# Stick-breaking masks as one row of four bf16 products ahead of the logits, and the bias tables' one-hot products as one row of three

## The chip, the cores and the metric

The kernel runs on one core of a Trainium2 chip. A core has a matrix engine (TensorE; the profile calls its products PE and its weight loads PEld), a vector engine (DVE), a scalar engine (ACT), GpSimd (POOL) and SyncE (SP), which issues transfers; POOL issues transfers too. The metric is the device time of one execution in microseconds (us); smaller is better. Each time is given beside runs of the kernel before on the same chip.

## The reference, cut to what matters

The program is one layer of a hybrid decoder over 512 tokens of width 1024: an input projection, three causal attention branches, gates, an output projection, a LayerNorm, a squared-ReLU MLP and a second LayerNorm. Two pieces of it are touched.

The stick-breaking branch has 8 heads of 64 columns. With z the scaled logits of query t and key s:

```python
before = k_pos[None, :] < q_pos[:, None]
log_keep = jnp.where(before, jax.nn.log_sigmoid(-z), 0.0)
later = lax.cumsum(log_keep, axis=3, reverse=True) - log_keep
a = jnp.where(before, jnp.exp(jax.nn.log_sigmoid(z) + later), 0.0)
```

The other two branches add a relative bias: a table `rel_bias` (32 buckets, 16 heads) is looked up at the bucket of the distance between query and key.

## The kernel before, in words

All large products run in a three-product form: a float32 operand is split into a high part, rounded to the format fp32r that TensorE takes, and a low part (the rest); high·high, high·low and low·high are summed in a bank of PSUM. The weights stream in through a ring: a DMA on SP (L213) brings raw rows, ACT casts the high part (`wh`, L243), DVE subtracts for the low part (`wl`, L245), and the projection items (`t_item`, `mm3`, L87 to L89) consume them. Two PSUM banks (`mm_bank`) alternate between items; six banks (`at_bank`) serve attention.

The main loop (L1965) walks over the items. Before an item's products, and once more in the middle of them, `step()` (L1937) advances the attention heads, which are Python generators, and then the pending generators, among them `tables()`. This gives the order in which instructions are written down; a planner of the framework then orders each engine's queue and allots buffers out of free pools, by data dependences and this order. `issue_after` adds ordering by hand in a few places.

**A stick-breaking head** (`sb_head`, L1601) takes three banks and writes four blocks of keys into them: block 3 (256 columns) and block 2 (256) share a bank, block 1 (384) and block 0 (512) have one each. For each block, from the last to the first, it issues the logits as two fp32r products (`mm_pair`, L146 and L147) and then one bf16 product identity × mask (L1613 with 256 columns for block 3, L1616 with 128 columns for the others), which adds -1e30 above the diagonal. So bf16 and fp32r products alternate. After that ACT and DVE form the log terms of each bank (L1628 to L1654), triangle and all-ones products add the sums over later keys in place (L1661, L1665), ACT takes the exponential (L1671), and value products write a fresh bank (L1684, L1686), which L1692 and L1693 take out. Eight heads run between 20 us and 229 us.

**The bias tables** (`rel_vec`, L1480, driven by `tables`, L1519): `make_lam` (L1562, at item 10) writes the bias table split into three bf16 parts, plus a row of -1e30, as `rel` (97 rows x 16). `load_onehot` brings three one-hot matrices `oh` (97 x 512, bf16). Five products follow, one in each step: `rel` columns of one head group (97 x 4) by 512, 128, 384, 256 and 256 columns of `oh` (L1483), each into a bank of its own, each copied out by ACT (L1485, 4 rows) and sent to a DRAM strip `rv` by a POOL DMA (L1486). Then `shifted` (L1489) reads `rv` back as shifted tables (L1495), and `turned` (L1505) reverses them at item 22.

Of the kernel before, what the change touches and what calls it, by code (L numbers as in the profile page):

```python
# [12 lines left out]
BF16 = mybir.dt.bfloat16  # L13
# [3 lines left out]
S = 512  # L17
D = 1024
P = 128
# [36 lines left out]
def trunk(tc, a, out):  # L56
    nc = tc.nc
    es = ExitStack()
    with es:
# [10 lines left out]
        def nm(s):  # L70
            uid[0] += 1
            return f"{s}_{uid[0]}"

        def slot(name, dt=F32):
            return big.tile([P, 512], dt, name=nm(name), tag="s", bufs=NSLOT)
# [4 lines left out]
        def mm_bank():  # L80
            return psum.tile([P, 512], F32, name=nm("mm"), tag="mm", bufs=2)

        def at_bank():
            return psum.tile([P, 512], F32, name=nm("at"), tag="at", bufs=6)
# [58 lines left out]
        def mm_pair(ps, st, tw, side, cs, cm, start, stop):  # L143

            hi, lo = tw[side]
            nc.tensor.matmul(ps, st[side][:, cs], hi[:, cm], start=start, stop=False, skip_group_check=True)  # L146
            nc.tensor.matmul(ps, st[side][:, cs], lo[:, cm], start=False, stop=stop, skip_group_check=True)  # L147
# [137 lines left out]
        T = {}  # L285
# [1162 lines left out]
        identb = one.tile([P, P], BF16, name="identb")  # L1448
# [13 lines left out]
        mask_b = one.tile([P, 2, P], BF16, name="mask_b")  # L1462
# [13 lines left out]
        rel = one.tile([97, 16], BF16, name="rel")  # L1476
        nc.vector.memset(rel[96:97, :], NEG)
        rv = dram.tile([16, 640], F32, name="rv")

        def rel_vec(cols, segs):  # L1480
            for src, d0, n in segs:
                ps = at_bank()
                nc.tensor.matmul(ps[0:4, :n], rel[:, cols], src, start=True, stop=True)  # L1483
                sb = slot("rvs")[0:4, :]
                nc.scalar.copy(sb[:, :n], ps[0:4, :n])  # L1485
                nc.gpsimd.dma_start(rv[cols, d0:d0 + n], sb[:, :n])  # L1486
                yield

        def shifted(h0, n, m):  # L1489
            ts = []  # L1490
            per = 512 // m
            for i in range(0, n, per):
                t = slot("sh")
                s = rv[h0 + i:h0 + i + 1, 0:1]
                nc.gpsimd.dma_start(t.rearrange("p (h m) -> p h m", m=m),  # L1495
                                    bass.AP(tensor=s.tensor, offset=s.offset,
                                            ap=[[1, P], [640, per], [1, m]]))
                ts.append(t)
            return ts, m
# [10 lines left out]
        tab_da = tab_g0 = tab_g1 = tab_g2 = None  # L1510

        oh = []

        def load_onehot():
            oh.extend(slot("oh", BF16) for _ in range(3))
            for i in range(3):
                nc.gpsimd.dma_start(oh[i][:97, :], a["onehot"][:, 512 * i:512 * i + 512])

        def tables():  # L1519
            nonlocal tab_g0, tab_g1, tab_g2  # L1520
            yield from rel_vec(slice(0, 4), [(oh[0][:97, :], 0, 512), (oh[1][:97, 0:128], 512, 128)])
            yield from rel_vec(slice(4, 8), [(oh[1][:97, 128:512], 0, 384)])
            yield from rel_vec(slice(8, 12), [(oh[2][:97, 0:256], 0, 256)])
            yield from rel_vec(slice(12, 16), [(oh[2][:97, 256:512], 0, 256)])
            tab_g0 = shifted(4, 4, 256)
            tab_g1 = shifted(8, 4, 128)
            tab_g2 = shifted(12, 4, 128)
# [34 lines left out]
        def make_lam():  # L1562
            lamt, t, r = lams

            nc.vector.tensor_copy(rel[0:32, :], t)
            nc.vector.tensor_sub(t, t, rel[0:32, :])
            nc.vector.tensor_copy(rel[32:64, :], t)
            nc.vector.tensor_copy(r, rel[32:64, :])
            nc.vector.tensor_sub(t, t, r)
            nc.vector.tensor_copy(rel[64:96, :], t)  # L1570
            lp = one.tile([P, 2], F32, name="lp")
            for i in range(2):
                nc.vector.scalar_tensor_tensor(lamt[:, 2 * i, :], lamt[:, 2 * i, :], 1.0, lamt[:, 2 * i + 1, :],
                                               op0=OP.mult, op1=OP.mult, accum_out=lp[:, i:i + 1])
            nc.scalar.activation(lp, lp, AF.Exp)
            nc.vector.tensor_sub(lam, lp[:, 0:1], lp[:, 1:2])
            nc.vector.tensor_scalar(lam, lam, LAM_INIT, -1.0, op0=OP.add, op1=OP.mult)
            nc.vector.tensor_scalar(gcol, gcol, 1.0 - LAM_INIT, None, op0=OP.mult)
# [22 lines left out]
        def sb_head(hd):  # L1601
            pr, side = hd // 2, hd % 2
# [3 lines left out]
            blk = [(0, 0, 0, 512), (1, 1, 0, 384), (2, 2, 0, 256), (3, 2, 256, 256)]  # L1606
            bank = [at_bank() for _ in range(3)]
            for kb, bi, c0, n in reversed(blk):
                ps = bank[bi][:, c0:c0 + n]
                mm_pair(ps, T["sb_k", pr], T["sb_q", pr], side, slice(kb * P, kb * P + P), slice(S - n, S),  # L1610
                        kb != 2, False)
                if kb == 3:
                    nc.tensor.matmul(ps, identb, mask_b.rearrange("p a b -> p (a b)"), start=False, stop=False,  # L1613
                                     skip_group_check=True)
                else:
                    nc.tensor.matmul(ps[:, 0:P], identb, mask_b[:, 1, :], start=False, stop=False,  # L1616
                                     skip_group_check=True)
            w = [512, 384, 512]
            sph, spl, later = {}, {}, {}
            for bi in (2, 1, 0):  # L1620
                n = w[bi]
                ps = bank[bi][:, :n]
# [35 lines left out]
            for kb, bi, c0, n in reversed(blk):  # L1658
                ps = bank[bi][:, c0:c0 + n]
                for hl in (sph, spl):  # L1660
                    nc.tensor.matmul(ps, tri_r, hl[bi][:, c0:c0 + n], start=False, stop=False, skip_group_check=True)  # L1661
                if kb < 3:
                    n2, hl = later[kb]
                    for t in hl:
                        nc.tensor.matmul(bank[bi][:, c0 + n - n2:c0 + n], ones_r, t, start=False, stop=False,  # L1665
                                         skip_group_check=True)
                if kb == 3:
                    continue
                n = w[bi]
# [12 lines left out]
            for kb, bi, c0, n in blk:  # L1682
                v = V["sb_v", 0, kb][hd // 4][:, hd % 4]
                nc.tensor.matmul(po[:, S - n:S], v.rearrange("p two d -> p (two d)"), ah[bi][:, c0:c0 + n],  # L1684
                                 start=kb == 0, stop=False, skip_group_check=True)
                nc.tensor.matmul(po[A, S - n:S], v[:, 0, :], al[bi][:, c0:c0 + n], start=False, stop=kb == 3,  # L1686
                                 skip_group_check=True)
# [233 lines left out]
        for hd in range(8):  # L1921
            waiting.append((3, sb_head(hd), SB_PERIOD))
# [42 lines left out]
        for n, it in enumerate(items):  # L1965
# [31 lines left out]
            if n == 10:  # L1997
                with tc.issue_after(st["low"]):
                    make_lam()
            if n == 9:  # L2000
                load_onehot()
            if n == 13:
                pending.append(tables())
# [33 lines left out]
            ps = it["bank"]() if it["bank"] else mm_bank()  # L2037
# [115 lines left out]
```

## Time and profile before

| what | value |
|---|---|
| time, median of 3 runs | 1042.58 us (1042.33 to 1043.28) |
| the profiled execution's own time | 1043.19 us |
| its span | 1041.0 us |
| TensorE products | 5450, each with a weight load of its own |
| share of the span, PE / PEld / DVE / ACT / POOL | 99% / 85% / 76% / 57% / 17% |
| mean granted TensorE clock | 0.998 of full speed |
| moved by DMA | 249.21 MB, mean 239 GB/s |

The span is what the profiler recorded between the first and the last instruction; 2.2 us of the execution lie outside it. A product's recorded duration is modelled and overlaps with the next one's (0.39 us for 512 columns, while one starts every 0.23 us), so what a product costs is read from the distance between starts, not from its duration. In rows of the timeline the first number is the start and the second the duration, both in us; then come engine, line, operation, output <- inputs, the tile (contraction rows * output rows), and the moved operand with its type. A wait that ended at another instruction stands in brackets.

### The profile page before, as it was taken

What the parts mean: (1) busy time and instruction counts of PE and PEld (TensorE: products, weight loads), DVE (VectorE), ACT (ScalarE), POOL (GpSimd) and SP (SyncE); (2) the same over time, 40 slices, a digit from 0 to 9 for tenths busy, and PEclk for the clock granted to TensorE, in tenths of its full rate; (3) what the DMA queues carried; (4) which work ended last, traced back from release to release, by engine and by line L of the source; (5) the groups of instructions that cost most, each with busy time, mean ns of one, the idle gap of its engine ahead of it and who ended that gap; (6) DMA issues with size and microseconds to landing.
All of it is one profiled execution on the core that took longest, in us unless ns stands there. A gap on an engine that the chain in (4) does not pass through costs nothing.

```text
span 1041.0 us, 15056 instructions
## 1 busy us (share of the span) xinstructions
PE 1031.1 (99%) x5450; PEld 880.1 (85%) x5450; DVE 787.0 (76%) x1408; ACT 593.2 (57%) x1014; POOL 180.0 (17%) x271
## 2 busy tenths in 40 slices
PE   9999999999999999999999999999999999999997
PEld 6888788889888888888888888889999889889886
DVE  6888577769774667779788895798768877877966
ACT  7566445536344545676575743775666556555651
POOL 0003412031211232411011040111111111111001
PEclk9999999999999999999999999999999999999999
DMA  8449978495985999967889795479999999999612
GB/s 308 121 154 271 255 214 197 128 283 142 278 207 206 258 281 294 248 199 202 251 238 230 269 320 197 147 219 331 320 288 316 296 316 314 306 344 286 201 59 81
DMA packets 71323, 249.21 MB, mean 239 GB/s; under 512 B 8809, under 2 KB 9593, under 8 KB 71249
## 3 DMA queue, kind: packets, MB, share of 16 engines
q0 software_dynamic: 32464, 116.21, 44.7%
q1 hardware_dynamic: 38208, 131.13, 35.2%
q8 instruction: 43, 0.70, 0.3%
q10 hardware_dynamic: 576, 0.92, 0.2%
q14 instruction: 32, 0.25, 0.1%
HBM read 246.10 MB, written 98.59 MB: 331 GB/s over the span
## 4 chain that ended last, share of the span: by engine, by line
PE 94%; DVE 2%; ACT 2%; issue 1%; DMA 0%; POOL 0%; DVEq 0%; POOLq 0%
PE mm L87 10%; PE mm L88 10%; PE mm L89 10%; PE at L1261 4%; PE at L1262 4%; PE at L1263 4%; PE at L599 3%; PE at L601 3%; PE at L600 3%; PE mm L496 2%; PE mm L498 2%; PE mm L497 2%; PE at L89 1%; PE at L87 1%; PE at L88 1%; PE at L761 1%
## 5 line engine op out<-in xcount | busy, mean ns | idle before, releaser
L243 ACT CAST wh<-raw 128x1024 fp32r<-128x1024 f32 x257 | 268.7, 1049 | 241.1 <-PE mm L88 133.6
L245 DVE TENSOR_TENSOR wl<-raw,wh 128x1024 fp32r<-128x1024 f32 x257 | 312.5, 1222 | 112.2 <-ACT wh L243 110.9
L87 PE MATMUL mm<-xhT,wh 128*128 128x512 f32 x302 | 120.0, 397 | 0.0
L89 PE MATMUL mm<-xhT,wl 128*128 128x512 f32 x302 | 118.3, 392 | 0.0
L88 PE MATMUL mm<-xlT,wh 128*128 128x512 f32 x302 | 118.2, 391 | 0.0
L87 PE MATMUL mm<-x1hT,wh 128*128 128x256 f32 x256 | 73.8, 288 | 0.0
L1261 PE MATMUL at<-wh,hh 128*128 128x512 f32 x188 | 73.7, 392 | 0.0
L1262 PE MATMUL at<-wl,hh 128*128 128x512 f32 x188 | 73.7, 392 | 0.0
L1263 PE MATMUL at<-wh,hl 128*128 128x512 f32 x188 | 73.1, 389 | 0.0
L88 PE MATMUL mm<-x1lT,wh 128*128 128x256 f32 x256 | 72.2, 283 | 0.0
L89 PE MATMUL mm<-x1hT,wl 128*128 128x256 f32 x256 | 71.8, 283 | 0.0
L89 PEld LDWEIGHTS mm<-xhT,wl 128*128 128x128 f32 x302 | 56.8, 188 | 12.0
L87 PEld LDWEIGHTS mm<-xhT,wh 128*128 128x128 f32 x302 | 56.8, 188 | 11.3 <-issue 0.4
L88 PEld LDWEIGHTS mm<-xlT,wh 128*128 128x128 f32 x302 | 56.8, 188 | 10.5
L87 PEld LDWEIGHTS mm<-x1hT,wh 128*128 128x128 f32 x256 | 48.8, 190 | 4.8 <-ACT up L1195 2.9
L88 PEld LDWEIGHTS mm<-x1lT,wh 128*128 128x128 f32 x256 | 48.9, 191 | 1.5
L89 PEld LDWEIGHTS mm<-x1hT,wl 128*128 128x128 f32 x256 | 48.6, 191 | 0.0
L1095 POOL DMA_DIRECT2D usum<-in_wu_dram x32 | 28.5, 928 | 103.1 <-DVE wl L245 38.7
L1095 POOL DMA_DIRECT2D dsum<-in_wd_dram x28 | 25.5, 933 | 100.2 <-DVE wl L245 33.3
L1263 PEld LDWEIGHTS at<-wh,hl 128*128 128x128 f32 x188 | 35.3, 188 | 7.6
L1261 PEld LDWEIGHTS at<-wh,hh 128*128 128x128 f32 x188 | 35.5, 189 | 6.0
L1262 PEld LDWEIGHTS at<-wl,hh 128*128 128x128 f32 x188 | 35.5, 189 | 5.6
(601 smaller groups left out, 2686.4 us busy)
## 6 DMA issues: line engine op xcount, KB each, us to landing
usum<-in_wu_dram POOLq DMA_DIRECT2D x48, 512.0 KB, 9.2
dsum<-in_wd_dram POOLq DMA_DIRECT2D x42, 512.0 KB, 9.1
raw<-in_wt_dram SPq DMA_DIRECT2D x38, 512.0 KB, 5.7
raw<-usum SPq DMA_DIRECT2D x32, 512.0 KB, 7.8
raw<-dsum SPq DMA_DIRECT2D x28, 512.0 KB, 8.1
raw<-in_wd_dram SPq DMA_DIRECT2D x25, 512.0 KB, 6.5
raw<-in_wu_dram SPq DMA_DIRECT2D x24, 512.0 KB, 7.2
raw<-in_wv_dram SPq DMA_DIRECT2D x18, 512.0 KB, 5.5
```

The lines of the kernel that those rows point to most:

```text
L87: nc.tensor.matmul(ps, wh, xh, start=start, stop=False, skip_group_check=True)
L88: nc.tensor.matmul(ps, wh, xl, start=False, stop=False, skip_group_check=True)
L89: nc.tensor.matmul(ps, wl, xh, start=False, stop=stop, skip_group_check=True)
L243: i = nc.scalar.copy(h, raw)
L245: i = nc.vector.tensor_sub(lo, raw, h.bitcast(F32))
L599: nc.tensor.matmul(ps, h[:, q], c["h"][:, n], start=go, stop=False, skip_group_check=True)
L600: nc.tensor.matmul(ps, h[:, q], c["l"][:, n], start=False, stop=False, skip_group_check=True)
L601: nc.tensor.matmul(ps, lo[:, q], c["h"][:, n], start=False, stop=end, skip_group_check=True)
L1095: i = nc.gpsimd.dma_start(o, i, accum_op=OP.add, max_dma_last_dim=4096)
L1261: nc.tensor.matmul(ps, h[:, q], c["h"][:, s], start=go, stop=False, skip_group_check=True)
L1262: nc.tensor.matmul(ps, h[:, q], c["l"][:, s], start=False, stop=False, skip_group_check=True)
L1263: nc.tensor.matmul(ps, lo[:, q], c["h"][:, s], start=False, stop=end, skip_group_check=True)
```

## The change

In `sb_head` the four mask products are issued first, in a row, into the still empty banks (the first one of each bank now clears it), and the eight logit products follow and add to them. The products and their shapes are the same.

The five one-hot products become three in a row into one bank. Their stationary operand is a padded copy of the table, `relp` (97 x 3 x 96, bf16, zero but for 16 columns in each third): product i multiplies all 512 columns of `oh[i]` and writes its 16 heads to rows 32i to 32i+15, adding zeros elsewhere. One ACT copy of 96 x 512 takes the bank out, and five POOL DMAs follow with the same pieces as before. The products stand in the third step of `tables` (before: one product in each of five steps), and `shifted` follows in the same step as before. `make_lam` gains four DVE instructions: a memset of `relp` and three copies of `rel` (97 x 16).

```diff
-        def rel_vec(cols, segs):
-            for src, d0, n in segs:
-                ps = at_bank()
-                nc.tensor.matmul(ps[0:4, :n], rel[:, cols], src, start=True, stop=True)
-                sb = slot("rvs")[0:4, :]
-                nc.scalar.copy(sb[:, :n], ps[0:4, :n])
-                nc.gpsimd.dma_start(rv[cols, d0:d0 + n], sb[:, :n])
-                yield
+        def rel_vec():
+            ps = at_bank()[0:96, :]
+            for i in range(3):
+                nc.tensor.matmul(ps, relp[0][:, i, :], oh[i][:97, :], start=i == 0, stop=i == 2)
+            sb = slot("rvs")[0:96, :]
+            nc.scalar.copy(sb, ps)
+            for i, g, c0, d0, n in ((0, 0, 0, 0, 512), (1, 0, 0, 512, 128), (1, 1, 128, 0, 384),
+                                    (2, 2, 0, 0, 256), (2, 3, 256, 0, 256)):
+                r = 32 * i + 4 * g
+                nc.gpsimd.dma_start(rv[4 * g:4 * g + 4, d0:d0 + n], sb[r:r + 4, c0:c0 + n])
...
         def tables():
-            yield from rel_vec(slice(0, 4), [(oh[0][:97, :], 0, 512), (oh[1][:97, 0:128], 512, 128)])
-            yield from rel_vec(slice(4, 8), [(oh[1][:97, 128:512], 0, 384)])
-            yield from rel_vec(slice(8, 12), [(oh[2][:97, 0:256], 0, 256)])
-            yield from rel_vec(slice(12, 16), [(oh[2][:97, 256:512], 0, 256)])
+            yield
+            yield
+            rel_vec()
+            for _ in range(3):
+                yield
...
+            relp.append(slot("relp", BF16)[:97, :288].rearrange("p (i c) -> p i c", i=3))
+            nc.vector.memset(relp[0], 0.0)
+            for i in range(3):
+                nc.vector.tensor_copy(relp[0][:, i, 32 * i:32 * i + 16], rel)
...
             for kb, bi, c0, n in reversed(blk):
-                ps = bank[bi][:, c0:c0 + n]
-                mm_pair(ps, T["sb_k", pr], T["sb_q", pr], side, slice(kb * P, kb * P + P), slice(S - n, S),
-                        kb != 2, False)
-                if kb == 3:
-                    nc.tensor.matmul(ps, identb, mask_b.rearrange("p a b -> p (a b)"), start=False, stop=False,
-                                     skip_group_check=True)
-                else:
-                    nc.tensor.matmul(ps[:, 0:P], identb, mask_b[:, 1, :], start=False, stop=False,
-                                     skip_group_check=True)
+                m = mask_b.rearrange("p a b -> p (a b)") if kb == 3 else mask_b[:, 1, :]
+                nc.tensor.matmul(bank[bi][:, c0:c0 + (n if kb == 3 else P)], identb, m, start=kb != 2, stop=False,
+                                 skip_group_check=True)
+            for kb, bi, c0, n in reversed(blk):
+                mm_pair(bank[bi][:, c0:c0 + n], T["sb_k", pr], T["sb_q", pr], side, slice(kb * P, kb * P + P),
+                        slice(S - n, S), False, False)
```

More of the change, by code (lines that the diff above doesn't have):

```diff
@@ L1512, in trunk @@
         oh = []
+        relp = []
         def load_onehot():
```

## The prediction

> **What bounds the kernel now.** I read the page first, then the waits of TensorE, then the timeline of TensorE and of its weight loads around one head and around the table products. From the page:
>
> ```profile
> PE 1031.1 (99%) x5450; PEld 880.1 (85%) x5450; DVE 787.0 (76%) x1408; ACT 593.2 (57%) x1014; POOL 180.0 (17%) x271
> PE 94%; DVE 2%; ACT 2%; issue 1%; DMA 0%; POOL 0%; DVEq 0%; POOLq 0%
> ```
>
> TensorE is busy in 99% of the span, and the chain that ended last runs 94% over it. Its waits, all of them:
>
> ```profile
> PE at L1440 <- DVE zero L1437: 1.2, 1, 1.2
> PE mm L690 <- DVE da_klb L101: 0.3, 1, 0.3
> PE at L887 <- ACT mh L798: 0.2, 1, 0.2
> PE mm L496 <- DVE sb_qlb L101: 0.2, 1, 0.2
> PE at L955 <- ACT ple L961: 0.2, 1, 0.2
> ```
>
> Nothing makes it wait for long between the first product and the last. Busy time hides small holes, though, since recorded durations overlap: only the distance of starts tells them. Head 4, with the product before it and the two after it, and three of its weight loads:
>
> ```profile
> 119.71 0.39 PE L89 MATMUL mm<-xhT,wl 128*128 128x512 f32 x1
> 119.94 0.28 PE L146 MATMUL at<-sb_qa,sb_ka 128*128 128x256 f32 x1
> 120.05 0.28 PE L147 MATMUL at<-sb_qla,sb_ka 128*128 128x256 f32 x1
> 120.18 0.28 PE L1613 MATMUL at<-mask_b,identb 128*128 128x256 bf16 x1
> 120.22 0.36 PE L146 MATMUL at<-sb_qa,sb_ka 128*128 128x256 f32 x1
> 120.42 0.28 PE L147 MATMUL at<-sb_qla,sb_ka 128*128 128x256 f32 x1
> ...
> 121.60 0.23 PE L1616 MATMUL at<-mask_b,identb 128*128 128x128 bf16 x1
> 121.64 0.47 PE L87 MATMUL mm<-xhT,wh 128*128 128x512 f32 x1
> 121.95 0.39 PE L88 MATMUL mm<-xlT,wh 128*128 128x512 f32 x1
> ```
>
> ```profile
> 120.17 0.10 PEld L1613 LDWEIGHTS <-identb 128*128 128x128 bf16 x1
> 120.18 0.20 PEld L146 LDWEIGHTS at<-sb_qa,sb_ka 128*128 128x128 f32 x1
> 120.30 0.19 PEld L147 LDWEIGHTS at<-sb_qla,sb_ka 128*128 128x128 f32 x1
> ```
>
> A 512-column fp32r product takes 0.23 us from start to start (119.71 to 119.94), a 256-column one 0.12 (119.94 to 120.05 and on to 120.18). The difference, 0.11 for 256 columns, is the rate of streaming: 0.43 ns a column, so 0.055 for 128. **A mask costs 0.12 us whatever its width**: from L1613 to the pair's second product are 0.24 us (120.18 to 120.42), of which that pair's first product would take 0.12; from the last L1616 to L88 are 0.35 (121.60 to 121.95), of which L87 takes 0.23. For 256 columns this is the streaming; a 128-column mask pays 0.065 more. The weight loads say why: the load for the pair behind the mask begins when the mask begins (120.18), and the next product's 0.12 later (120.30). I read it as: behind a mask, TensorE is held for one fp32r load of about 0.12, and a mask shorter than this hides only part of it.
>
> **The masks in a row.** Before: 4 x 0.12 = 0.48 us a head. After: the first mask (256 columns) 0.12; the two in the middle are followed by a bf16 load, not by an fp32r one; the last is followed by fp32r and costs 0.12 again. No warm row shows a bf16 product behind a bf16 product. The nearest below is the bare stream, 0.055; the nearest above is the mask as it stands, 0.12. I take 0.06, next to the stream, because the bf16 load is recorded at 0.10 against 0.20 for fp32r. That makes 0.12 + 2 x 0.06 + 0.12 = 0.36, 0.12 less a head and **0.96 less in 8 heads**; the ends are 0 and 8 x 2 x 0.065 = 1.04. The eight logit products keep their number, shapes and partners, and cost what they did.
>
> The TensorE page of the Trainium skill ("TensorE: Matmul & The Clock Gate", Back-to-back issue gap) gives about 81 ns for each of a stream of weight load and 128-column product pairs; by this the masks would save 8 x 2 x (0.12 - 0.081) = 0.62, an estimate, and the time below would be 0.34 higher. No run here shows it yet.
>
> **The tables in a row.** The first and the last of the five products, and the row for all five:
>
> ```profile
> 99.06 0.34 PE L1665 MATMUL at<-sml,ones_r 128*128 128x384 f32 x1
> 99.33 0.38 PE L1483 MATMUL at<-oh,rel 97*4 97x512 bf16 x1
> 99.64 0.50 PE L87 MATMUL mm<-xhT,wh 128*128 128x512 f32 x1
> 99.97 0.39 PE L88 MATMUL mm<-xlT,wh 128*128 128x512 f32 x1
> ...
> 113.08 0.39 PE L89 MATMUL mm<-xhT,wl 128*128 128x512 f32 x1
> 113.40 0.27 PE L1483 MATMUL at<-oh,rel 97*4 97x256 bf16 x1
> 113.60 0.50 PE L87 MATMUL mm<-xhT,wh 128*128 128x512 f32 x1
> 113.94 0.40 PE L88 MATMUL mm<-xlT,wh 128*128 128x512 f32 x1
> ```
>
> ```profile
> L1483 PE MATMUL at<-oh,rel x5: 218/271/377, 99.3 to 113.4; 97*4 97x256 bf16 x2, 97*4 97x512 bf16 x1, 97*4 97x128 bf16 x1, 97*4 97x384 bf16 x1
> ```
>
> The first one stretches its neighbourhood to 0.91 us (99.06 to 99.97); L1665 (384 columns, 0.18) and L87 (0.23) explain 0.41, so it costs 0.50. The last: 0.86 less 2 x 0.23 is 0.40. Less the stream (0.22 for 512, 0.11 for 256) both leave about 0.285, paid on the way in and out. Five products: 512 + 128 + 384 + 256 + 256 = 1536 columns at 0.43 ns, 0.66 us, and 5 x 0.285 = 1.43: 2.09 us. After, three products stream 3 x 512 = 1536 columns, the same 0.66, and pay the way in and out once: 0.95. **Saved: 4 x 0.285 = 1.14 us.** If each of the three still pays it, only 2 x 0.285 = 0.57 is saved; if the wider shape (96 columns of weights instead of 4) pays no more than a mask, 0.12, then 1.31.
>
> **What goes to other engines.** DVE gains a memset and three copies behind the last write of `rel`, in front of an evacuation that frees a bank for the next item:
>
> ```profile
> 68.57 0.17 DVE L1570 CAST rel<-lamt 32x16 bf16<-32x16 f32 x1
> 69.48 0.69 DVE L101 SCALAR_TENSOR_TENSOR sb_qlb<-mm,sb_qb 64x512 fp32r<-64x512 f32 x1
> 72.10 0.47 PE L87 MATMUL mm<-xhT,wh 128*128 128x512 f32 x1
> L1437 DVE MEMSET zero<- x1: 272/272/272, 0.9 to 0.9; 128x256 uint32 x1
> ```
>
> Three copies of 0.17 and at most one 0.27 memset are 0.78 us. L101 ended at 70.17, and the item that takes the bank began at 72.10, behind head 2: 1.9 us of cover, of which 1.1 stay. I cost it at nothing; without cover it would be up to 0.78. ACT drops four small copies and is not the bound. POOL issues the five strips behind one copy near 108 us, where the old ones went out between 102 and 117; what stands behind them in its queue is the sums that the value items read much later:
>
> ```profile
> L1095 POOL DMA_DIRECT2D vsum<-in_wv_dram x4: 828/833/1214, 81.6 to 108.2; - x4
> L213 SPq DMA_DIRECT2D raw<-vsum x4: 326/326/330, 191.9 to 239.2; - x4
> ```
>
> Five issues of about 0.8 us (the first row's duration) delay them by 4 us at most; the first read is 84 us after the last of these issues. SP's own queue is not touched. What is late next is nothing up to 229 us, and the rest of the saving has to pass the short waits at L690, L887 and L955.
>
> **The sum.** 0.96 + 1.14 = 2.10 us less, all of it on TensorE, which the chain follows to the end. The profiled execution took 1043.19 us (span 1041.0 and 2.2 outside it), so such an execution would take 1041.1. It stands 0.61 above the median of the runs, 1042.58; from the median the forecast is **1040.5 us**. The ends of the two terms together give 0.57 to 2.4 less: 1042.0 to 1040.2.
>
> **Rivals.**
> (a) *A row doesn't help*: every bf16 product goes on to wait for its own load, or the planner pulls the row apart. Then the masks save nothing and the tables 0.57: 1042.0. For it speaks the only bf16 row in the trace, at the start, beside the clock there:
>
> ```profile
> L1440 PE MATMUL at<-zero x9: 608/634/634, 1.2 to 4.6; 128*128 128x512 bf16 x9
> 1.20:5.30 4.10, 4.02 (x9) 1.19 (x9) 0.41 (x2) 1.85 (x4) 1.16 (x5) 1.00 0.77 234
> ```
>
> Eight steps in 3.4 us are 0.43 us for 512 columns, nearly twice the later 0.23, at a granted clock of 1.00. Against it: the fp32r rows overlap their loads, and I see no reason for bf16 ones not to. The same page (Part 1) has a cold array run at half rate in its first microseconds, 426.7 ns for 512 columns; by this the start-up row would hold no load time at all, but the clock column does not show it.
>
> (b) *Slower: a mask waits for a bank.* TensorE's queue is in order, and the masks now need all three banks within 0.24 us of the head's first product, where the last bank, block 0's, was first touched by the pair that ends at 121.60, two 512-column products and a held load earlier (2 x 0.23 + 0.07), 1.1 us after 119.94: now some 0.88 us earlier. If a bank is freed in that time, the whole queue stands behind the mask. Priced at the full 0.88 in all 8 heads it is 7.0 us, and 1047.5 in sum; from 0.53 a head (4.2 us) on the kernel is slower by over 0.2%. For it: banks come from a free pool that the planner deals out, and one table bank now replaces five. Against it, the tightest case that I find, the bank that head 0's output left before head 2:
>
> ```profile
> 67.28 0.68 DVE L1693 TENSOR_TENSOR oT<-at,ot 64x512 f32<-64x512 f32 x1
> 70.40 0.28 PE L146 MATMUL at<-sb_qa,sb_ka 128*128 128x256 f32 x1
> ```
>
> It was free at 67.96, 2.4 us before the first product.
>
> (c) *Swallowed*: a later wait grows by what is gained, and the time stays at 1042.6. The waits behind 240 us sum to 0.7 us (L690, L887, L955), so other engines are ahead almost everywhere.
>
> (d) *More than the sum*: the planner, with eight free products at hand, also closes other holes, as at 31 us (L496 waiting); 1039.5 or less.
>
> **Chances.** Forecast case, 1.6 to 2.4 us less, 0.55: it straddles the limit, 0.36 beyond 0.2% and 0.19 short of it. (a) 0.14 and (c) 0.05: within. (b), with other orders that cost, 0.17: slower. (d) 0.09: faster. So faster by over 0.2% 0.45, within 0.2% 0.38, slower 0.17; 0.2% is 2.09 us, about what a measurement of this kernel can tell from no change. The forecast's own range is 1040.2 to 1041.0; with (a), (c), most of (d) and half of (b) the range is 1039.3 to 1045.0.
>
> **What would show it.** Right: in the new timeline, masks stand four in a row 0.055 to 0.065 apart, with the row's cost at 0.36; three L1483-like products 0.22 to 0.23 apart, way in and out together near 0.285; TensorE's waits unchanged. Wrong: steps of 0.08 to 0.12 between masks (the load of a bf16 product isn't hidden), an idle TensorE in front of the first or second mask with a release by ACT or DVE (b), masks torn apart by other products, or a new wait behind 229 us of the size of the gain (c).

## The result, and the profile after

| | time, median | ratio to before, 95% interval |
|---|---|---|
| before | 1043.04 us (1042.33 to 1043.54, 8 runs) | |
| after | 1040.11 us (1039.74 to 1040.59, 8 runs) | 0.9971 [0.996, 0.9981] |

The change saves 2.93 us, 0.29%; the interval's near end is at 0.19%. The profiled execution of after took 1040.08 us with a span of 1038.1, the one of before 1043.19 with 1041.0.

The page of after, its engine line and its chain; then the waits of TensorE (engine and line that waited, the releaser, sum in us, count, longest):

```profile
PE 1028.0 (99%) x5448; PEld 881.2 (85%) x5448; DVE 787.0 (76%) x1412; ACT 591.7 (57%) x1010; POOL 180.1 (17%) x271
PE 94%; DVE 2%; ACT 1%; DMA 1%; issue 1%; SPq 0%; POOL 0%; DVEq 0%; ACTq 0%; POOLq 0%
```

```profile
PE at L1440 <- DVE zero L1437: 1.2, 1, 1.2
PE at L146 <- ACT wh L243: 0.4, 1, 0.4
PE mm L690 <- DVE da_klb L101: 0.3, 1, 0.3
PE at L887 <- ACT mh L798: 0.2, 1, 0.2
PE at L955 <- ACT ple L961: 0.2, 1, 0.2
```

The bound is the same: TensorE, 99% busy, 94% of the chain. Its busy time is 3.1 us shorter, the span 2.9. Of the waits, the one at L496 isn't there and one at L146 (at 21 us, in head 0) is; experiment 6 shows that this swap is chance and no part of the change. The three late ones are what they were.

Head 4 in the timeline of TensorE of after, with the product before the row, and then its weight loads (a row marked x4 holds four instructions in sequence; its duration reaches from the first's start to the last's end):

```profile
117.49 0.39 PE L89 MATMUL mm<-xhT,wl 128*128 128x512 f32 x1
117.72 0.45 PE L1618 MATMUL at<-mask_b,identb 128*128 128x256 bf16 x4
117.98 0.36 PE L146 MATMUL at<-sb_qa,sb_ka 128*128 128x256 f32 x1
118.18 0.28 PE L147 MATMUL at<-sb_qla,sb_ka 128*128 128x256 f32 x1
```

```profile
117.71 0.28 PEld L1618 LDWEIGHTS <-identb 128*128 128x128 bf16 x4 [0.26 <-issue]
117.95 0.19 PEld L146 LDWEIGHTS at<-sb_qa,sb_ka 128*128 128x128 f32 x1
118.06 0.19 PEld L147 LDWEIGHTS at<-sb_qla,sb_ka 128*128 128x128 f32 x1
```

The first mask starts 0.23 behind L89, so nothing is paid on the way in. From it to L147 are 0.46 us, of which L146 (256 columns) takes 0.12: **the row costs 0.34 us**, where four masks cost 0.48 before. Heads 1 to 7 all show the same 0.46. The row of masks ends at 118.17; the last, of 128 columns, lasts 0.22, so it starts at 117.95, and 0.23 is left for the three steps: 0.12 for the 256 columns and 0.055 for each of the inner two, the bare stream. What is left is held on the way out: L147 comes 0.20 behind L146 instead of 0.12, as behind a single mask before.

The tables in the timeline of after, products and loads together:

```profile
105.33 0.28 PE L1691 MATMUL at<-al,sb_v 128*64 128x256 f32 x1
105.33 0.45 PEld L1483 LDWEIGHTS <-relp 97*96 97x96 bf16 x3
105.44 0.81 PE L1483 MATMUL at<-oh,relp 97*96 97x512 bf16 x3
...
105.87 0.19 PEld L87 LDWEIGHTS mm<-xhT,wh 128*128 128x128 f32 x1
105.90 0.59 PE L87 MATMUL mm<-xhT,wh 128*128 128x512 f32 x1
...
106.33 0.40 PE L88 MATMUL mm<-xlT,wh 128*128 128x512 f32 x1
```

From L1691 (0.12) to L88, less L87 (0.23), are 0.65 to 0.66 us: **three streams of 0.22 and nothing on the way in or out**. By the same reading (distance of starts around a product, less the steps of its neighbours) the five products of before cost 0.50, 0.36, 0.46, 0.41 and 0.41, in sum 2.14. So the products themselves give 1.48.

Where the time went along TensorE: the start of one and the same product in each trace, less its start in before. The second and third columns are of experiments 1 and 2, the fourth of experiment 7.

| product, its start in before | after | masks only | tables only | row turned |
|---|---|---|---|---|
| L496, 31.49 us | -0.16 | -0.51 | -0.36 | +0.08 |
| behind head 2, 72.41 | -0.40 | -0.77 | -0.41 | -0.20 |
| behind head 3, 95.30 | -0.53 | -0.91 | -0.40 | -0.38 |
| behind the tables, 116.50 | -2.22 | -0.92 | -2.09 | -2.07 |
| behind head 4, 121.95 | -2.37 | -1.07 | -2.09 | -2.27 |
| behind head 5, 146.31 | -2.52 | -1.22 | -2.09 | -2.48 |
| behind head 6, 170.67 | -2.67 | -1.37 | -2.09 | -2.68 |
| behind head 7, 195.03 | -2.83 | -1.53 | -2.09 | -2.89 |
| the last product, 1033.45 | -2.94 | -1.46 | -1.89 | -2.87 |

A reader can follow the whole gain here: 0.37 in heads 1 to 3, 1.69 over the tables, 0.15 in each of heads 4 to 7, and then 800 us in which nothing is given back. The first row isn't part of it: profiles differ there by some tenths before any touched instruction has mattered, as experiment 6 shows.

### The profile page after: what moved, and what is told of

It reads as the page before. It is cut to its first block, busy times and chain, and to the rows that moved or that the text cites. A ratio compares the mean times of both kernels' runs of the same rounds, so it can differ in the third digit from the quotient of the medians.

```text
span 1038.1 us, 15050 instructions
## 1 busy us (share of the span) xinstructions
PE 1028.0 (99%) x5448; PEld 881.2 (85%) x5448; DVE 787.0 (76%) x1412; ACT 591.7 (57%) x1010; POOL 180.1 (17%) x271
## 4 chain that ended last, share of the span: by engine, by line
PE 94%; DVE 2%; ACT 1%; DMA 1%; issue 1%; SPq 0%; POOL 0%; DVEq 0%; ACTq 0%; POOLq 0%
PE mm L87 10%; PE mm L88 10%; PE mm L89 10%; PE at L1261 4%; PE at L1262 4%; PE at L1263 4%; PE at L599 3%; PE at L600 3%; PE at L601 3%; PE mm L496 2%; PE mm L498 2%; PE mm L497 2%; PE at L89 1%; PE at L88 1%; PE at L87 1%; PE at L761 1%
## 5 line engine op out<-in xcount | busy, mean ns | idle before, releaser
L87 PE MATMUL mm<-xhT,wh 128*128 128x512 f32 x302 | 119.1, 394 | 0.0
L89 PE MATMUL mm<-xhT,wl 128*128 128x512 f32 x302 | 118.2, 391 | 0.0
L88 PE MATMUL mm<-xlT,wh 128*128 128x512 f32 x302 | 118.1, 391 | 0.0
L87 PE MATMUL mm<-x1hT,wh 128*128 128x256 f32 x256 | 73.7, 288 | 0.0
L88 PE MATMUL mm<-x1lT,wh 128*128 128x256 f32 x256 | 72.2, 283 | 0.0
L89 PE MATMUL mm<-x1hT,wl 128*128 128x256 f32 x256 | 71.8, 283 | 0.0
L89 PEld LDWEIGHTS mm<-xhT,wl 128*128 128x128 f32 x302 | 56.8, 188 | 11.9
L87 PEld LDWEIGHTS mm<-xhT,wh 128*128 128x128 f32 x302 | 56.7, 188 | 11.0
L88 PEld LDWEIGHTS mm<-xlT,wh 128*128 128x128 f32 x302 | 56.7, 188 | 10.8
L87 PEld LDWEIGHTS mm<-x1hT,wh 128*128 128x128 f32 x256 | 48.7, 190 | 4.8 <-ACT up L1195 3.0
L88 PEld LDWEIGHTS mm<-x1lT,wh 128*128 128x128 f32 x256 | 48.8, 191 | 1.5
L89 PEld LDWEIGHTS mm<-x1hT,wl 128*128 128x128 f32 x256 | 48.6, 191 | 0.0
```

The source lines that it names most:

```text
L87: nc.tensor.matmul(ps, wh, xh, start=start, stop=False, skip_group_check=True)
L88: nc.tensor.matmul(ps, wh, xl, start=False, stop=False, skip_group_check=True)
L89: nc.tensor.matmul(ps, wl, xh, start=False, stop=stop, skip_group_check=True)
```

## The experiments

**Theory.** L: an fp32r product behind a bf16 mask is held until its own weight load of about 0.12 us is through, so the last mask before an fp32r product costs the greater of its stream and 0.12, and a mask before another mask costs its stream. N: table products with few weight columns pay about 0.3 us in and out, which wide weights don't. **Rivals.** S: each change between the two kinds of product has a fixed price, whatever the widths; for the tables, that it is the row that saves, not the width; and that the two parts of the change don't add.

### 1 and 2: each part alone

Masks only has the table code of before; tables only has the mask code of before:

```diff
-            rel_vec()                                          # masks only
+            yield from rel_vec(slice(0, 4), [...])             # and three more, as before
```

```diff
-            for kb, bi, c0, n in reversed(blk):                # tables only
-                nc.tensor.matmul(bank[bi][...], identb, m, start=kb != 2, ...)
...
+                mm_pair(ps, ..., kb != 2, False)               # then its mask, as before
```

> Only the masks stand in a row; the five table products are as before. Theory L (the fp32r product behind a mask is held for one weight load of about 0.12 us, so a mask costs the longer of its stream and 0.12, and only the last of a row pays): 0.34 us a head instead of 0.48, 0.14 x 8 = 1.1 us less, less 0.4 for the wait that head 0 got, plus 0.3 for the hole before L496 near 31 us that closed: about 1.0 us less than before, near 1042.0. Rival S (every change of number format costs a fixed 0.05 to 0.07 beside the stream) gives the same here. Rival P (most of the gain comes from another order that the planner happened to choose, not from the rows themselves): the masks alone and the tables alone do not add up to the 2.9 us of the whole change.

Measured: 1041.57 us (1041.15 to 1042.24, 11 runs), ratio 0.9987 [0.9978, 0.9996].

> Only the table products are changed; masks and logits alternate as before. From the trace of the whole change: the row of three takes 0.66 us where the five took 2.09, 1.4 us less, and the products around them gain some 0.2 more: 1.4 to 1.7 less, near 1041.5. With masks_only this should add up to 2.4 to 2.9. Under rival P it doesn't.

Measured: 1041.23 us (1040.76 to 1042.38, 11 runs), ratio 0.9985 [0.9976, 0.9993]; before, for both, 1042.85. The gains, 1.28 and 1.62, add to 2.90; the whole gives 2.93. The table above says it more sharply: masks only gains 0.15 in each of heads 4 to 7 and 0.01 over the tables, tables only 1.69 over the tables and nothing in heads 4 to 7. From 31 us to 195 us masks only gains 1.02. So the parts add, and the rival that they don't is out.

### 3: is it the row, or the width of the weights?

Wide, apart: the masks and the five places of before, but 96 weight columns (16 filled, the rest zeros that nobody reads). Narrow, in a row: three products by all 16 columns of `rel`, in the one step of after, masks as before.

```diff
-                nc.tensor.matmul(ps[0:4, :n], rel[:, cols], src, start=True, stop=True)
+                nc.tensor.matmul(ps[0:96, :n], relp[0], src, start=True, stop=True)       # wide, apart
```

```diff
-                nc.tensor.matmul(ps, relp[0][:, i, :], oh[i][:97, :], start=i == 0, stop=i == 2)
+                nc.tensor.matmul(ps[i], rel, oh[i][:97, :], start=True, stop=True)        # narrow, in a row
```

> Five separate table products in five steps, as before, but with weights padded with zeros to 96 columns (97 x 96 instead of 97 x 4). Theory W (the way in and out, 0.285 us a product, comes from the narrow weights): it is gone although the products stay apart; the distance around each shrinks to its stream or to at most 0.12, 1.2 to 1.4 us less in sum, near 1041.7. Rival R (a row pays it once, whatever the weights): each product still costs 0.285 beside its stream, time as before, 1043.0.

> Three table products in a row as in the change, but with the unpadded table as weights (97 x 16 instead of 97 x 96), each into a bank of its own, three copies instead of one. Theory W: each of the three pays its way in and out: 0.66 + 3 x 0.285 = 1.5 us in place of 2.09, 0.6 less than before. Rival R: paid once, 0.95 us, 1.1 less than before. Read from the distance between the starts around the row.

Measured: wide, apart 1040.87, narrow, in a row 1041.83 (one execution each; before 1042.85). Timelines of TensorE around the first table product of wide, apart, and then of its loads:

```profile
98.39 0.34 PE L1669 MATMUL at<-sml,ones_r 128*128 128x384 f32 x1
98.57 0.38 PE L1483 MATMUL at<-oh,relp 97*96 97x512 bf16 x1
98.60 0.59 PE L87 MATMUL mm<-xhT,wh 128*128 128x512 f32 x1
99.03 0.40 PE L88 MATMUL mm<-xlT,wh 128*128 128x512 f32 x1
```

```profile
98.39 0.12 PEld L1483 LDWEIGHTS <-relp 97*96 97x96 bf16 x1
98.57 0.19 PEld L87 LDWEIGHTS mm<-xhT,wh 128*128 128x128 f32 x1
```

The same two views of narrow, in a row:

```profile
105.40 0.28 PE L1689 MATMUL at<-al,sb_v 128*64 128x256 f32 x1
105.61 0.60 PE L1483 MATMUL at<-oh,rel 97*16 97x512 bf16 x2
106.14 0.50 PE L87 MATMUL mm<-xhT,wh 128*128 128x512 f32 x1
106.48 0.40 PE L88 MATMUL mm<-xlT,wh 128*128 128x512 f32 x1
```

```profile
105.61 0.10 PEld L1483 LDWEIGHTS <-rel 97*16 97x16 bf16 x2 [0.18 <-issue]
106.14 0.19 PEld L87 LDWEIGHTS mm<-xhT,wh 128*128 128x128 f32 x1 [0.43 <-issue]
```

Here the wide weights are loaded one product ahead: the load stands at 98.39, its product at 98.57, on time, 0.18 behind L1669, and L88 comes 0.64 behind L1669 (0.18 + 0.22 + 0.23 would be 0.63). The five wide products cost 0.23, 0.12, 0.17, 0.11 and 0.12, in sum 0.75: **the width alone gives 1.39 of the 1.48, the row the last 0.09**. The execution of wide, apart is ahead of before by more than these 1.39, since its starts are 0.65 ahead at 31 us already, by chance. In the narrow row the first load starts only with its product, 0.09 late (105.61 where 105.40 + 0.12 was due), and L87's load begins only behind the row's stream. The row of two costs 0.74 (1.08 from L1689 to L88, less 0.12 and 0.23): 0.44 of stream and 0.30 paid once. A row does save where the weights are narrow; the order of the queue tore the third product off, though, which cost 0.51 by itself, so the sum is 1.24. This is neither the 1.5 of theory W nor the 0.95 of its rival: each narrow row pays once, as the rival has it, but there were two rows. For wide weights theory W holds.

### 4: at which width does it stop?

```diff
-            relp.append(slot("relp", BF16)[:97, :96])                # of wide, apart
+            relp.append(slot("relp", BF16)[:97, :64])                # and :32
```

> The order of before with all five table products 97 x 32 instead of 97 x 4 or 97 x 16 (padding by columns that nobody reads). With 4 and 16 columns a product between two projection products paid about 0.3 us in and out; with 96 it paid none. Theory N (narrow weights aren't loaded ahead of their product; the bound lies between 16 and 32 columns): five products cost about 0.75 us in sum. Rival (the bound lies above 32 columns): about 2.1 us, as in the kernel before. The masks are as in the change or as in before, which does not touch this sum.

> The same with 97 x 64. The value products' weights have 64 columns and stand between fp32r products with their loads taken one product ahead, so theory N expects 64 columns to be free of the way in and out: five products at about 0.75 us in sum. Rival (only weights near the full width are loaded ahead): about 2.1 us.

Measured: 1043.58 and 1043.01 us (one execution each; before 1042.98); the five products cost 2.19 and 2.27 us in sum, as in before. One of those with 64 columns, products and then loads:

```profile
106.90 0.28 PE L1690 MATMUL at<-al,sb_v 128*64 128x256 f32 x1
107.11 0.35 PE L1483 MATMUL at<-oh,relp 97*64 97x384 bf16 x1
107.39 0.50 PE L87 MATMUL mm<-xhT,wh 128*128 128x512 f32 x1
107.73 0.40 PE L88 MATMUL mm<-xlT,wh 128*128 128x512 f32 x1
```

```profile
106.79 0.13 PEld L1690 LDWEIGHTS at<-al,sb_v 128*64 128x64 f32 x1
107.11 0.11 PEld L1483 LDWEIGHTS <-relp 97*64 97x64 bf16 x1 [0.18 <-issue]
107.39 0.19 PEld L87 LDWEIGHTS mm<-xhT,wh 128*128 128x128 f32 x1 [0.17 <-issue]
```

Theory N missed: 64 columns pay like 4. So it isn't the padded copy as such that made the wide products cheap. The price can be taken apart here: 0.09 on the way in (0.21 behind L1690 instead of 0.12), 0.11 on the way out (L87 0.28 behind 384 columns instead of 0.17), and 0.11 that L88 is held (0.34 instead of 0.23). It isn't the width alone either: in the same lines the value product L1690, fp32r with 64 columns, has its load one product ahead. So bf16 weights of 97 rows with 4, 16, 32 or 64 columns pay, 96 don't, and fp32r with 64 doesn't. Why is not settled.

### 5: what holds the product behind a mask?

Both keep the order and the tables of before. One widens the 128-column masks to 256 (128 columns of zeros are added); the other makes mask and identity fp32r.

```diff
-                    nc.tensor.matmul(ps[:, 0:P], identb, mask_b[:, 1, :], start=False, ...)
+                    nc.tensor.matmul(ps[:, 0:2 * P], identb, mask_b[:, 1:3, :].rearrange(...), start=False, ...)
```

```diff
-        identb = one.tile([P, P], BF16, name="identb")
+        identb = one.tile([P, P], F32R, name="identb")
-        mask_b = one.tile([P, 2, P], BF16, name="mask_b")
+        mask_b = slot("mask_b", F32R)[:, :2 * P].rearrange("p (a b) -> p a b", a=2)
```

> Masks alternate with logits and tables are as before, but each of the 128-column masks is widened to 256 columns with zeros (the added columns change nothing in the sum). Theory L: a mask costs the longer of its stream (0.11) and the held load (0.12), so a widened mask still costs 0.12 and the time is that of before, 1043.0. Rival S: a fixed cost beside the stream, so 24 masks cost 0.055 more each, 1.3 us more in sum, 1044.3.

> Masks alternate as before, but identity and mask are fp32r like the logits, so there is no change of number format; tables as before. Theory L: a 128-column mask is still too short to hide the next load: 0.11 to 0.12 each, time as before within 0.3 us, 1042.7 to 1043.0. Rival S: no change of format, no cost beside the stream: 24 masks at 0.055 instead of 0.12 and 8 at 0.11, 1.6 us less, 1041.4.

Measured: 1043.52 and 1042.97 (one execution each; before 1042.93). A widened mask before a pair of 512 columns, in the timeline of TensorE, and then an fp32r mask:

```profile
121.42 0.28 PE L1617 MATMUL at<-mask_b,identb 128*128 128x256 bf16 x1
121.46 0.47 PE L146 MATMUL at<-sb_qa,sb_ka 128*128 128x512 f32 x1
121.77 0.39 PE L147 MATMUL at<-sb_qla,sb_ka 128*128 128x512 f32 x1
```

```profile
120.97 0.22 PE L1616 MATMUL at<-mask_b,identb 128*128 128x128 f32 x1
121.03 0.44 PE L146 MATMUL at<-sb_qa,sb_ka 128*128 128x512 f32 x1
121.31 0.39 PE L147 MATMUL at<-sb_qla,sb_ka 128*128 128x512 f32 x1
```

From the mask to L147 are 0.35 us with 256 columns, 0.12 beside the 0.23 of L146, where the prediction read 0.12 with 128 columns: twice the stream costs nothing more. With fp32r throughout there is no change of kind, and the mask still costs 0.34 - 0.23 = 0.11. In the starts along TensorE the widened masks move nothing in heads 4 to 7 (+0.40 at 116.50 and at 195.03), the fp32r ones 0.03 a head. By S the first would have lost about 1.3 us and the second gained about 1.6. S fails at both, by the starts; the two times, of one execution each, could not show it, since the runs of before beside them lie between 1042.58 and 1043.61. **What holds is a floor of 0.11 to 0.12 for a product with an fp32r product behind it**, and the kind of the short product matters for 0.01. That this floor is the weight load is read from the rows: behind the row of masks, L146's load starts with the last mask (117.95) and L147's 0.11 later (118.06). The recorded duration of such a load, 0.19 to 0.20, is longer than the floor.

### 6: the wait in head 0

In after the masks of head 0 stand ahead of two projection products, and L146 waits 0.36 us for `wh`. Here head 0 begins with the pair of block 3 again:

```diff
+            first = hd == 0
+            if first:
+                kb, bi, c0, n = blk[3]
+                mm_pair(bank[bi][:, c0:c0 + n], ..., True, False)
```

> The whole change, but in head 0 alone the first logit pair is issued ahead of the masks. In the change, head 0's masks went ahead of two projection products and its first logit product then waited 0.36 us. Theory: the planner pulls forward whatever is ready, masks need nothing but a bank, and TensorE then stands before the logits; with the pair first the two products go back ahead and the wait is gone: 0.3 to 0.45 us less than the change, near 1039.7. Rival: the two products only move behind and the time stays within 0.1 of the change, 1040.1.

> The kernel before, once more, for a second profile. In the first profile of before and that of the change TensorE's first products differ by 0.23 us by 7 us already, with the same order on its queue. If that is chance (arrival of the first transfers), this profile differs by as much from the first one; if it belongs to the change, this profile equals the first one within 0.05 us at 16 us.

Measured: 1040.32 us (1039.96 to 1040.75, 10 runs), ratio 0.9975 [0.9966, 0.9985], not faster than after's 1040.11. The two projection products did go back ahead of the logits, but the wait stayed: in this profile L146 waits 0.35 us for `wh` as well. So the theory failed in its first step, that the masks make the wait; what the wait costs was not tested. Before, once more, took 1044.30 in one execution. Two of its waits:

```profile
PE at L761 <- DVE b L772: 0.7, 1, 0.7
PE at L146 <- ACT wh L243: 0.3, 1, 0.3
```

The first stands at 558 us, far from the change, and shows how much a single profile can carry by chance; the second profile of after has it too (0.4). The second line is the wait that the profile of after has, here in the kernel without the change. Each of the 14 profiles has either this wait at L146 or the one at L496, never both: the first profile of before has L496 and the second L146, the first of after L146 and the second L496. Neither belongs to the change.

The beginning of before, once more, shows the same scatter: its first products at 7 us stand 0.72 ahead of the first profile of before, at 21 us 0.23 behind, at 31 us 0.07 ahead. Over all profiles the start at 31 us lies between 0.65 ahead and 0.64 behind, and in most of them what differs there stays to the end. The mask row of head 0, worth 0.14, can't be read against that in the starts or the time. What happens at 31 us in after and then in before:

```profile
31.33 0.47 PE L496 MATMUL mm<-wh,xhT 128*128 128x512 f32 x1
```

```profile
31.49 0.47 PE L496 MATMUL mm<-wh,xhT 128*128 128x512 f32 x1 [0.23 <-DVE sb_qlb L101]
```

L496 starts 0.16 earlier and doesn't wait. Tables only, with the masks of before, has -0.36 there and waits, so this is no part of the change either.

### 7: the row turned round

If only the last mask of a row is held, the widest should stand last. The reordered kernel, and after once more on the same chip:

```diff
-            for kb, bi, c0, n in reversed(blk):
+            for kb, bi, c0, n in blk:
...
-                nc.tensor.matmul(bank[bi][...], identb, m, start=kb != 2, stop=False,
+                nc.tensor.matmul(bank[bi][...], identb, m, start=kb != 3, stop=False,
```

> The change with the row of masks turned round: the three masks of 128 columns first, the one of 256 columns last, just ahead of the logits. Theory L (a logits product of fp32r behind a mask is held until its own weight load of about 0.12 us is through, so the last mask of the row costs the greater of its stream and 0.12; the others cost their bare stream): 3 x 0.055 + 0.12 = 0.285 us a head instead of 0.34, eight times 0.055 less, so 1039.7 us beside about 1040.1 of the change. Rival S (a fixed cost of about 0.06 to 0.07 for each change from one kind of product to the other, whatever stands last): a row costs the same in any order, 1040.1 us. What tells them apart is the distance from the first mask to the first logits product of heads 1 to 7, 0.285 against 0.34 (by L counted as distance less 0.12 of the logits product before it), and the offset at 229 us, since 0.4 us is near what the times can tell.

> The changed kernel once more, for the comparison with the turned row on the same chip: 1040.1 us, within 0.4, a row of masks at 0.34 us a head and three table products in a row at 0.66 us. Both theories expect the same of it.

Measured: turned 1039.92 us (1039.30 to 1040.21, 6 runs), ratio 0.9969 [0.9958, 0.9981]; after 1040.12 (1039.70 to 1041.14, 8 runs), ratio 0.9974 [0.9963, 0.9984]. The times alone can't separate them. The timeline of TensorE of the turned row can:

```profile
117.87 0.45 PE L1618 MATMUL at<-mask_b,identb 128*128 128x128 bf16 x4
118.08 0.36 PE L146 MATMUL at<-sb_qa,sb_ka 128*128 128x256 f32 x1
118.28 0.28 PE L147 MATMUL at<-sb_qla,sb_ka 128*128 128x256 f32 x1
```

From the row's start to L147 are 0.41 instead of 0.46, in each of heads 1 to 7, so the row costs 0.29, and the table of starts gives 0.20 to 0.21 for each of heads 4 to 7 instead of 0.15. L said 0.285 and 0.055 less a head; S said no change. That is L again, now as a prediction of something not yet run. The other sign that was named, the offset at 229 us, tells nothing: turned is ahead of before by 2.90 there and the first profile of after by 2.84, because turned was 0.24 behind after at 31 us. Over heads 4 to 7 alone the starts of turned gain 0.82 and those of after 0.61. The medians differ by 0.2 where L said 0.4, which is within their scatter.

## Why the prediction was right or wrong

The forecast was 1040.5, measured 1040.11: inside the range, and 0.1 below the forecast's own range. The gain was larger than forecast, 2.93 against 2.10. That the time came closer than the gain is luck: before stood at 1042.58 in the first three runs and at 1043.04 in the eight beside after.

- **Bound, and that a gain on TensorE reaches the end: right.** The starts stay 2.8 to 2.9 us earlier from 195 us to the last product, past L690, L887 and L955 with unchanged waits. Rival (c) is out.
- **A mask costs 0.12 whatever its width, because a load holds the next product: right.** Experiments 5 and 7 show the floor of 0.11 to 0.12 and that it falls on the last of a row; that a load makes it is read from the loads' starts.
- **Masks in a row, 0.36 a head: right in kind, a little small.** I took 0.06 for an inner mask and measured 0.055; the row costs 0.34. The saving is 0.14 to 0.15 a head in heads 4 to 7 and 0.12 in heads 1 to 3, 0.98 us in seven heads by the starts, against 0.96 forecast for eight; head 0 can't show it in the first profile, but in the second one of after its row takes 0.46 like the others. The rule of the Trainium skill ("TensorE: Matmul & The Clock Gate", Back-to-back issue gap), about 81 ns for a load and a 128-column product, isn't borne out in these rows of four: with 0.055 measured, the 0.62 that I estimated from it is too small.
- **The tables: wrong in the step "three products stream 3 x 512 = 1536 columns, the same 0.66, and pay the way in and out once: 0.95".** With 96 columns of weights they pay nothing and cost 0.66. I had the wider shape as a bound ("no more than a mask, 0.12, then 1.31"), and even this bound fell short: 1.48 in the products themselves. The cause was wrong as well: the forecast has a row save four of five ways in and out, but padding alone, with no row, gives 1.39. So the sum was too small by its second term, 1.14 where the starts show 1.69.
- **What the 0.285 left out.** Over the tables the starts move by 1.69, 0.21 more than the products' own cost shows; in wide, apart by 1.59, 0.20 more. So it goes with the narrow products too, some 0.04 each: the projection products behind one follow each other at 0.23 to 0.24 for some ten steps, where they otherwise keep to 0.227. By which mechanism isn't shown.
- **DVE, POOL and SP at nothing: right.** The copies of `rel` didn't even stand where I had put them, at 68 us, but at 83; nobody waits for them, and the sums that POOL issues come and are read as before:

```profile
L1578 DVE COPY relp<-rel x3: 164/164/172, 83.0 to 83.2; 97x16 bf16<-97x16 bf16 x3
...
L1095 POOL DMA_DIRECT2D vsum<-in_wv_dram x4: 823/831/1214, 81.3 to 106.8; - x4
...
L213 SPq DMA_DIRECT2D raw<-vsum x4: 326/326/331, 189.2 to 236.3; - x4
```

- **Rival (a)** is out (the rows of experiments 1 to 3). The slow bf16 row that spoke for it tells nothing of bf16 loads: the first fp32r products are as slow (last section). **Rival (b)**: no mask waits for a bank; the first one of head 4 starts on time, and the waits of TensorE name none. **Rival (d)**: not needed; the hole at L496 comes and goes by chance (experiment 6).

In sum by the starts: 0.98 for the masks and 1.69 for the tables are 2.67; 0.16 at 31 us and 0.11 behind 195 us, in steps that no run ties to the change, make up the rest of 2.94 in these two profiles.

## What to carry to other kernels

Before a short product is costed, look at what stands behind it in the queue: here the 0.055 us of streaming was hidden in a 0.12 us load, so putting short products together, by the starts best with the longest last, saved what making them shorter could not: 128 columns cost what 256 did. Where a product with a few weight columns stands among full ones, look at the distance of the starts around it: if more is paid than its stream, try padding with unread zero columns. Here 96 columns were worth more than a row, while 32 and 64 saved nothing. And when a part of a change has two features (here a row and a wider shape), price them apart, since the forecast gave the whole gain to the wrong one.

## What the runs showed that was not expected

- bf16 weights of 97 rows and 4 to 64 columns cost 0.3 us in and out between fp32r products, those with 96 columns none (0.75 against 2.14 to 2.27 us for the five), though more is loaded; fp32r weights with 64 columns pay nothing in the same place.
- The load of the 128-column identity (bf16) also starts only with its product (117.71 for 117.72), and yet delays it by nothing: the mask stands 0.23 behind L89. So "not loaded ahead" alone doesn't set the price; 0.09 and 0.11 of the narrow ones' price have another cause that these runs don't name.
- Four bf16 products with a load each follow one another at the bare stream, 0.055 us for 128 columns, where the nearest row of before, nine such products at 1 to 5 us, had 0.43 for 512, twice the stream. The kind of the products doesn't make those early steps: in the same profile the fp32r products that start at 5.95, 6.38 and 6.81 us are 0.43 apart as well, and from 7.07 us on they keep to 0.23. These pairs of before show it:

```profile
6.38 0.86 PE L347 MATMUL at<-xhT,wl 128*128 128x512 f32 x2
7.07 0.63 PE L347 MATMUL at<-xlT,wh 128*128 128x512 f32 x2
7.54 0.63 PE L347 MATMUL mm<-xhT,wh 128*128 128x512 f32 x2
```

The first pair takes 0.69 to the next one's start, the second 0.47. What ends the slow stretch isn't shown here; the granted clock is 1.00 in it and behind it.
